# Where the later conditioning rows are kept, and which tile pairs are turned by transfers, in a conditioned decoder layer

## The chip, the cores and the metric

The kernel runs on one core of a Trainium2 chip. Its engines work side by side: TensorE (PE) multiplies, VectorE (DVE) and ScalarE (ACT) work on elements, GpSimd (POOL) only issues a few transfers, and SyncE (SP) issues nearly all transfers from HBM. Each engine takes its own instructions in order and waits on semaphores for the others. The metric is the time of one execution in microseconds on the device. Three executions of the kernel before took 2380.26, 2380.55 and 2392.89 us: the median is 2380.55 us. All of it is measured with the kernel's weights in float32.

## The reference, cut to what matters

One layer over 256 tokens of width 2048: a SwiGLU feed-forward, a pair of token mixers (retention, and attention in a window), and a second SwiGLU feed-forward, each behind an RMS norm. The norms are shifted and scaled, and the results gated, by nine vectors that come from a condition `c`.

```python
c_act = silu(c)
mod = (c_act @ w_ada + b_ada).reshape(1, 9, 2048)      # nine vectors, 151 MB of weights
h = modulate(rms_norm(x, norm_ffn1), mod[:, 0], mod[:, 1])
x = x + 0.5 * mod[:, 2] * swiglu(h, w_ffn1_gu, w_ffn1_down)      # 2048 -> 2 x 5632 -> 2048
h = modulate(rms_norm(x, norm_mix), mod[:, 3], mod[:, 4])
x = x + mod[:, 5] * token_mixing(h, w_in, w_ret_branch, w_swa_branch, w_out, sinks)
h = modulate(rms_norm(x, norm_ffn2), mod[:, 6], mod[:, 7])
x = x + 0.5 * mod[:, 8] * swiglu(h, w_ffn2_gu, w_ffn2_down)
return rms_norm(x, norm_final)

def token_mixing(h, ...):
    rq, rk, rv, rg, sq, sk, sv, gl_ret, gl_swa = split(h @ w_in)
    y_ret = (silu(rg) * group_rms(retention(rotary(rq), rotary(rk), rv))) @ w_ret_branch
    y_swa = windowed_attention_with_sinks(sq, sk, sv) @ w_swa_branch
    return (sigmoid(gl_ret) * y_ret + sigmoid(gl_swa) * y_swa) @ w_out
```

## The kernel before

**Products.** Every matrix product is made in three matmuls of a reduced float32 format: the float32 operand is split into a high half and the rest, and high x high, low x high and high x low are added up in PSUM (L338, L339, L341 in `products`). The 256 tokens are two tiles of 128. A weight block of four times 128 x 512 (1 MB) is loaded into one of four buffers called `raw` (`load`, L328; L964 in the first feed-forward's first part). `split` makes its halves two chunks at a time: ScalarE casts the high half `wh` (L351), VectorE subtracts to get `wl` (L353). One weight block is two splits and 24 matmuls. `gemm_part` walks one block for each column group; `gemm` goes over all of K.

**Order.** SP's queue is in the order of the code. The other engines' instructions are ordered by a scheduler ahead of time, except in two stretches whose order is written by hand. A `raw` buffer is loaded again when VectorE has made the second `wl` of the block that was in it, four loads earlier.

**Conditioning rows.** `c_act @ w_ada` is not done on TensorE. The weights lie transposed, and a row is 128 x 2048 (1 MB): 128 outputs. VectorE multiplies it with `c_act` and sums, in four passes of 512 (`ada_pass`, L206). There are 144 rows, 16 for each vector. `conditioning` is a generator with one pass a step; `tick`, called for each half block, runs it at the rate that `set_pace` sets. A row's place comes from `place()`, and its load (`ada_load`, L201) is put into SP's queue `pace["ahead"]` passes ahead of its first pass. There are two kinds of places. `raw_row` takes the next of the four `raw` buffers, the ring of the weights. `two_rows` takes a big buffer (a `slot`, 2 MB) and uses its two halves in turn. The first feed-forward uses `raw_row` in its last group, and then two halves of a slot, at 1.37 passes for each half block and four passes ahead. The token mixers and the second feed-forward use `raw_row`, two passes ahead; behind the softmax heads the rate is 0.95, in the second feed-forward 64/160 = 0.4.

**Tiles that are turned.** After a SwiGLU pair (one gate and one up product of 512 columns) the result must be transposed to be the next product's operand. `transpose_to` does this on TensorE, four 128 x 128 transposes for each of two token tiles (L479), and ScalarE copies them out of PSUM (L480). `turn_by_dma` does it by transfer: ScalarE copies the two 16-bit halves of the words apart (L496), SP issues a transposing transfer (L501), and ScalarE puts the halves together (L512). `later` spreads these steps over ten blocks; `turn_step` runs one step of each open turn after each block.

**Stages,** with the start of the first load of each in the profiled execution: the first feed-forward's first eight pairs of columns in four groups over K (its last group, the only one with turned pairs, is issued from about 290 us on), its last three pairs from 372 us, its down projection from 499 us, the projection to the mixers from 731 us (first keys and values, then queries, rotary and values, with the softmax heads and the retention as side work, then gates and `rg`), the branch projections with gates from 1274 us, `w_out` from 1547 us, the second feed-forward's up projection to 2120 us, and its down projection to the end. `soft`, which holds the logits of the softmax heads, lies in the place of `x_sb` (tag `x`); x is written to HBM before (`x_d`, L1051) and read back by POOL (L1376) when the place is free.

Of the kernel before, what the change touches and what calls it, by code (L numbers as in the profile page):

```python
# [9 lines left out]
F32 = mybir.dt.float32  # L10
# [7 lines left out]
P = 128  # L18
S = 256
D = 2048  # L20
DFF = 5632
# [3 lines left out]
CH = 512  # L25
# [3 lines left out]
EARLY = 8  # L29
# [48 lines left out]
def layer_kernel(  # L78
# [25 lines left out]
    one = ctx.enter_context(tc.tile_pool(name="one", bufs=1))  # L104
# [33 lines left out]
    def slot():  # L138
        return slots.tile([P, KD * S], F32, tag="slot", name=nm("slot"))
# [55 lines left out]
    AQ = 4  # L195
# [33 lines left out]
        raw = raws.tile([P, KB, CH], F32, tag="raw", name=nm("raw"))  # L229
        return raw.rearrange("p k n -> p (k n)")  # L230

    def two_rows():

        both = slot()
        turn = [both[:, :D], both[:, D:]]

        def place():
            turn.append(turn.pop(0))
            return turn[-1]

        return place
# [59 lines left out]
    turns = []  # L301
# [581 lines left out]
    gu, dn = w_ffn1_gu[0], w_ffn1_down[0]  # L883
# [125 lines left out]
    for g, ks in enumerate(groups):  # L1009
        final = g == len(groups) - 1  # L1010
        if final:
            set_pace(ROWS_FFN1, 32 * 192 // 32, place_row, 1)
        order = chunks if (len(groups) - g) % 2 else chunks[::-1]
        coming = iter(()) if final else group(groups[g + 1])
        due = 0 if final else 2 * len(groups[g + 1])
        stay = () if final else order[-2:]
        for i, n in enumerate(order):
            visit(n, ks, n not in stay, final)
            if final:
                turn_step()  # L1020
            last = len(order) - 2
            for _ in range((i + 1) * due // last - i * due // last if i < last else i == last):
                next(coming, None)
            if n in stay:
                continue
            if not final:
                to_parts(n)
            elif n % 2:
                swiglu_up(
                    banks.pop(n - 1),  # L1030
                    banks.pop(n),
                    tiles,
                    n // 2,
                    (part_of(n - 1), part_of(n)),
                    n // 2 in (1, 5),
                )
    gate = gate_row()
    tiles.append(slot())
    row_ring.append(two_rows())
    pace["rate"] = (192 - 32) / 117  # L1040
    pace["ahead"] = AQ
    ffn_up(held, gu, tiles, EARLY, turned=range(EARLY, DFF // CH - 1))
    gate_in = gate_load(gate, 2)
    wi = w_in[0]
    held, head, ahead, *calls = into_norm(3, wi, O_SK, O_SV)
# [6 lines left out]
    soft = one.tile([P, NT * D], F32, tag="x", name="soft")  # L1052
    planes_of = one.tile([P, D], F32, tag="row", name="planes_of")
    RATE_SOFT, RATE_AFTER = 0.25, 0.95
    set_pace([(7, 2, None), (6, None, None), (5, None, 1.0)], 192 / 0.95, raw_row, 2)

    def in_chunk(c0):
        return gemm(held, wi, [c0])[0]
# [142 lines left out]
    def softmax_heads():  # L1201

        turned = {}
        for at in range(4 * (QUADS + 1) + 2):
            g, part = divmod(at, 4)
            if part == 0 and g < QUADS:
                quad_weights(g)
            if part == 1 and g >= 2:
                quad_values(g - 2)
            if part == 2 and g >= 1:  # L1210
                turned[g - 1] = quad_turn()
            if part == 2 and g < QUADS:
                quad_apart()
            if part == 3 and g >= 1:
                quad_together(turned.pop(g - 1))
                if g == QUADS:
                    dec.append(one.tile([P, D], F32, tag="row", name="dec"))
                    nc.gpsimd.dma_start(dec[0], consts[:, C_DEC:])
            yield
        pace["rate"] = RATE_AFTER  # L1220

    for ci in range(4):
        b = in_chunk(O_SQ + ci * CH)
# [157 lines left out]

    gate = gate_row()
    tiles = [slot() for _ in range(3)]
    set_pace([(8, None, 0.5)], 160, raw_row, 2)
    ffn_up(held, w_ffn2_gu[0], tiles, 0, head, range(DFF // CH - 1), ahead)
    gf = one.tile([P, KD * S], F32, tag="hh", name="gf")[:, :D]
    spare = one.tile([P, 2, KD * P], F32R, tag="hl", name="spare")
    nc.gpsimd.dma_start(gf, norm_final[None, :].broadcast_to([P, D]))
# [107 lines left out]
```

## Time and profile before

| what | value |
|---|---|
| three runs, median | 2380.55 us (2380.26 to 2392.89) |
| profiled execution | 2393.78 us; span of the core 2392.0 us, mean granted clock 0.997 |
| TensorE busy | 2351.4 us |
| VectorE / ScalarE busy | 1702.1 / 1310.0 us |
| moved by DMA | 625.78 MB, 262 GB/s in the mean |
| rows loaded into `raw` / into a slot (1 MB each) | 73 / 67, landing 5.5 / 7.1 us after issue (median) |
| transposing transfers at L501 | 62, landing 6.6 us after issue (median) |
| transposes on TensorE at L479 | 72 |

In rows of instructions stand the line, the engine, the operation, out<-in by the program's names, the count, then busy time in us and mean ns of one, and then the idle time of the engine before them with what ended it. In rows of a timeline the first number is the start in us from the span's start, the second the duration, and a bracket tells how long the engine stood idle before and what released it. In rows of waits stand the total in us, the number of waits and the longest. In rows by window stand the window, its length, the busy time of PE, of its weight loads, of DVE, ACT and POOL with counts, the granted clock, the DMA engines' busy share, and GB/s. The chain that ended last is almost wholly TensorE's matmuls at L338, L339 and L341.

### The profile page before, as it was taken

The page shows a single profiled execution, that of the slowest core. Times are in us where ns is not written, and L with a number is a line of the kernel's source. Part 1 is how long each engine was busy: PE and PEld are TensorE (multiplying, and loading weights), DVE is VectorE, ACT ScalarE, POOL GpSimd, SP SyncE. Part 2 cuts the span into 40 slices and gives each one's busy share as a digit, 9 for nine tenths or more (in the row PEclk, how much of TensorE's full clock was granted, in tenths as well). Part 3 has the DMA queues.
Part 4 walks back from the last instruction along what each step waited for, and adds up shares of the span by engine and source line. Part 5 has one row for each costly group of instructions (what it writes and reads, how often), then busy time and mean ns, then how long its engine had stood idle before and what let it go on. Part 6 is the DMA issues. An engine that isn't in the chain of part 4 may idle for free. (4 is left out here: it accounts for less than half of the span.)

```text
span 2392.0 us, 28418 instructions
## 1 busy us (share of the span) xinstructions
PE 2351.4 (98%) x10470; PEld 1924.5 (80%) x10470; DVE 1702.1 (71%) x2635; ACT 1310.0 (55%) x1792; POOL 7.7 (0%) x18
## 2 busy tenths in 40 slices
PE   7999999999999999999999999999999999999998
PEld 5788888888788888778887787887888888888886
DVE  6887799778877768976776676767655555545656
ACT  6553456454546568774555464466445445454544
POOL 0000000000000000000000000000000000000000
PEclk9999999999999999999999999999999999999999
DMA  9977789998876789867689797755667877765553
GB/s 354 367 278 277 265 284 342 349 339 316 321 255 236 279 270 247 253 213 286 248 278 293 236 299 282 272 195 192 237 238 237 254 247 246 255 220 194 183 204 124
DMA packets 177581, 625.78 MB, mean 262 GB/s; under 512 B 100321, under 2 KB 100705, under 8 KB 106913
## 3 DMA queue, kind: packets, MB, share of 16 engines
q1 hardware_dynamic: 175362, 613.11, 74.4%
q0 software_dynamic: 1504, 9.81, 1.0%
q8 instruction: 82, 1.34, 0.2%
q10 hardware_dynamic: 576, 1.05, 0.1%
q14 instruction: 57, 0.47, 0.1%
HBM read 597.16 MB, written 4.22 MB: 251 GB/s over the span
## 5 line engine op out<-in xcount | busy, mean ns | idle before, releaser
L351 ACT CAST wh<-raw 128x1024 fp32r<-128x1024 f32 x794 | 834.0, 1053 | 927.1 <-PE pa L339 895.4
L353 DVE TENSOR_TENSOR wl<-raw,wh 128x1024 fp32r<-128x1024 f32 x794 | 964.2, 1223 | 524.6 <-ACT wh L351 522.3
L338 PE MATMUL pa<-wh,hh 128*128 128x512 f32 x2192 | 855.4, 391 | 3.3 <-ACT wh L351 3.3
L339 PE MATMUL pa<-wh,hl 128*128 128x512 f32 x2192 | 854.5, 390 | 0.2 <-DVE hl L601 0.2
L341 PE MATMUL pa<-wl,hh 128*128 128x512 f32 x2192 | 778.2, 392 | 1.4 <-DVE wl L353 1.3
L338 PEld LDWEIGHTS pa<-wh,hh 128*128 128x128 f32 x2192 | 411.9, 188 | 93.6 <-ACT wh L351 5.3
L341 PEld LDWEIGHTS pa<-wl,hh 128*128 128x128 f32 x2192 | 409.9, 188 | 90.4 <-DVE wl L353 4.3
L339 PEld LDWEIGHTS pa<-wh,hl 128*128 128x128 f32 x2192 | 412.1, 188 | 85.2 <-DVE hl L601 0.4
L339 PE MATMUL pa<-wh,a 128*128 128x512 f32 x944 | 365.8, 390 | 0.4 <-DVE a L387 0.4
L341 PE MATMUL pa<-wl,a 128*128 128x512 f32 x944 | 351.0, 392 | 9.4 <-DVE wl L353 9.4
L338 PE MATMUL pa<-wh,a 128*128 128x512 f32 x944 | 350.7, 392 | 1.7 <-DVE t L607 1.1
L206 DVE CUSTOM_DVE_ANT_0 raw<-raw,cact 128x512 f32<-128x512 f32 (+1 forms) x296 | 189.8, 695 | 65.5 <-DMA raw<-in_w_ada_dram 59.4
L341 PEld LDWEIGHTS pa<-wl,a 128*128 128x128 f32 x944 | 177.3, 188 | 49.9 <-DVE wl L353 13.5
L338 PEld LDWEIGHTS pa<-wh,a 128*128 128x128 f32 x944 | 178.0, 189 | 40.3 <-DVE t L607 1.9
L339 PEld LDWEIGHTS pa<-wh,a 128*128 128x128 f32 x944 | 177.8, 188 | 37.9 <-DVE a L387 1.0
L206 DVE CUSTOM_DVE_ANT_0 slot<-slot,cact 128x512 f32<-128x512 f32 (+1 forms) x216 | 170.0, 835 | 5.1 <-DMA slot<-in_w_ada_dram 4.8
L512 ACT COPY slot<-back 128x512 uint16<-128x512 uint16 x124 | 82.7, 766 | 0.0
L387 DVE TENSOR_TENSOR a<-slot,a 128x512 fp32r<-128x512 f32 x118 | 80.5, 684 | 0.0
L386 ACT CAST a<-slot 128x512 fp32r<-128x512 f32 x118 | 72.7, 617 | 1.9 <-DVE t L671 1.9
L496 ACT COPY flat<-t 128x512 uint16<-128x512 uint16 x112 | 63.5, 616 | 8.1 <-DVE t L1344 5.5
L206 DVE DVE_READ_ACCUMULATOR2_ANT sums<- 128x1 f32 x512 | 42.2, 82 | 0.0
L996 DVE TENSOR_TENSOR slot<-slot,pa 128x512 f32<-128x512 f32 x48 | 31.9, 683 | 3.2 <-PE pa L341 3.1
(205 smaller groups left out, 1143.1 us busy)
## 6 DMA issues: line engine op xcount, KB each, us to landing
raw<-in_w_ffn_gu_dram SPq DMA_DIRECT2D x160, 1024.0 KB, 5.2
raw<-in_w_in_dram SPq DMA_DIRECT2D x104, 1024.0 KB, 5.7
raw<-in_w_ffn_down_dram SPq DMA_DIRECT2D x88, 1024.0 KB, 4.9
raw<-in_w_ada_dram SPq DMA_DIRECT2D x73, 1024.0 KB, 5.5
slot<-in_w_ada_dram SPq DMA_DIRECT2D x67, 1024.0 KB, 7.1
raw<-in_w_ffn_gu_dram SPq DMA_DIRECT2D x32, 512.0 KB, 5.5
raw<-in_w_swa_branch_dram SPq DMA_DIRECT2D x16, 1024.0 KB, 5.1
raw<-in_w_ret_branch_dram SPq DMA_DIRECT2D x16, 1024.0 KB, 5.0
```

The lines of the kernel that those rows point to most:

```text
L206: nc.vector.tensor_tensor_reduce(out=w[:, at], in0=w[:, at], in1=cact[:, at], scale=1.0, scalar=0.0, op0=ALU.mult, op1=ALU.add, accum_out= ...
L338: nc.tensor.matmul(ps, ah[:, j, ts], wh[:, j, :], start=first, stop=False)
L339: nc.tensor.matmul(ps, al[:, j, ts], wh[:, j, :], start=False, stop=False)
L341: nc.tensor.matmul(ps, ah[:, j, ts], wl[:, j, :], start=False, stop=last).ins
L351: cast.append(nc.scalar.copy(hi, src).ins)
L353: low.append(nc.vector.tensor_sub(lo, src, hi.bitcast(F32)).ins)
L386: nc.scalar.copy(hi, v)
L387: nc.vector.tensor_sub(lo, v, hi.bitcast(F32))
L496: nc.scalar.copy(planes[:, i, :], words(src)[:, :, i])
L512: nc.scalar.copy(into[:, :, :, i], held["turned"][:, i])
L996: nc.vector.tensor_add(p, p, b)
```

## The change

There are three parts.

- *More turned pairs.* In the first feed-forward's last group the pairs 1, 3, 5 and 7 are turned by transfers, where it was 1 and 5; of the pairs 8, 9 and 10 behind it all three, where it was 8 and 9; in the second feed-forward all eleven, where it was the first ten. So four pairs, with 32 transposes, leave TensorE, and eight transposing transfers are added.
- *Rows of the mixers.* Behind the softmax heads (which end in the projection `w_in`), after seven more blocks and in the step of the eighth, a tile `rows_x` is made in the place of `soft`, and rows go to its two halves, loaded four passes ahead. Until then they use the `raw` ring as before. The rate is the same.
- *Rows of the second feed-forward.* They go to two halves of the fourth slot, four passes ahead, at 64/150 = 0.427 a half block and starting five passes' worth later.

```diff
-    def two_rows():
-
-        both = slot()
+    def two_rows(both=None):
+
+        both = slot() if both is None else both
...
-                    n // 2 in (1, 5),
+                    n // 2 % 2 == 1,
...
-    ffn_up(held, gu, tiles, EARLY, turned=range(EARLY, DFF // CH - 1))
+    ffn_up(held, gu, tiles, EARLY, turned=range(EARLY, DFF // CH))
...
-    set_pace([(7, 2, None), (6, None, None), (5, None, 1.0)], 192 / 0.95, raw_row, 2)
+    row_ring.clear()
+    set_pace([(7, 2, None), (6, None, None), (5, None, 1.0)], 192 / 0.95, place_row, 2)
+
+    def rows_beside():
+
+        for _ in range(7):
+            yield
+        row_ring.append(two_rows(one.tile([P, 2 * D], F32, tag="x", name="rows_x")))
+        pace["ahead"] = AQ
...
         pace["rate"] = RATE_AFTER
+        turns.append(rows_beside())
...
-    set_pace([(8, None, 0.5)], 160, raw_row, 2)
-    ffn_up(held, w_ffn2_gu[0], tiles, 0, head, range(DFF // CH - 1), ahead)
+    set_pace([(8, None, 0.5)], 150, two_rows(), AQ)
+    pace["due"] = -5.0
+    ffn_up(held, w_ffn2_gu[0], tiles, 0, head, range(DFF // CH), ahead)
```

**Where instructions move.** First, SP's queue in the first feed-forward, where the last group ends and the next part begins (`in_w_ffn_gu` are weight blocks, `in_w_ada` rows). Before:

```order
L964 DMA raw_2920<-in_w_ffn_gu_dram 128x2048
L964 DMA raw_2958<-in_w_ffn_gu_dram 128x2048
L201 DMA raw_2993<-in_w_ada_dram 128x2048
L964 DMA raw_3027<-in_w_ffn_gu_dram 128x2048
L964 DMA raw_3068<-in_w_ffn_gu_dram 128x2048
L201 DMA raw_3103<-in_w_ada_dram 128x2048
L328 DMA raw_3133<-in_w_ffn_gu_dram 128x2048
L201 DMA slot_3130<-in_w_ada_dram 128x2048
```

The same place after the change:

```order
L964 DMA raw_2914<-in_w_ffn_gu_dram 128x2048
L964 DMA raw_2952<-in_w_ffn_gu_dram 128x2048
L201 DMA raw_2987<-in_w_ada_dram 128x2048
L964 DMA raw_3021<-in_w_ffn_gu_dram 128x2048
L501 DMA_TRANSPOSE back_3057<-flat_2792 128x8x128
L964 DMA raw_3064<-in_w_ffn_gu_dram 128x2048
L201 DMA raw_3099<-in_w_ada_dram 128x2048
L501 DMA_TRANSPOSE back_3102<-flat_2857 128x8x128
L328 DMA raw_3119<-in_w_ffn_gu_dram 128x2048
L201 DMA slot_3116<-in_w_ada_dram 128x2048
```

The two transfers of pair 3 now stand between the weight blocks, one ahead of the last row of the ring and one ahead of the first row of the slot.

Second, SP's queue in the branch projections, for the same weight blocks and the same row (`raw_10521` before; after, the second row of `rows_x` shown). Before:

```order
L328 DMA raw_10400<-in_w_swa_branch_dram 128x2048
L201 DMA raw_10435<-in_w_ada_dram 128x2048
L328 DMA raw_10442<-in_w_swa_branch_dram 128x2048
L501 DMA_TRANSPOSE back_10478<-flat_10269 128x8x128
L328 DMA raw_10486<-in_w_swa_branch_dram 128x2048
L201 DMA raw_10521<-in_w_ada_dram 128x2048
L501 DMA_TRANSPOSE back_10524<-flat_10310 128x8x128
```

After (`raw_10436` is the block that was `raw_10442`):

```order
L201 DMA rows_x<-in_w_ada_dram 128x2048
L328 DMA raw_10396<-in_w_swa_branch_dram 128x2048
L328 DMA raw_10436<-in_w_swa_branch_dram 128x2048
L201 DMA rows_x<-in_w_ada_dram 128x2048
L501 DMA_TRANSPOSE back_10473<-flat_10265 128x8x128
L328 DMA raw_10481<-in_w_swa_branch_dram 128x2048
L501 DMA_TRANSPOSE back_10517<-flat_10307 128x8x128
```

The row's load moves ahead of one weight block and one transposing transfer, and the weight blocks have the four `raw` buffers to themselves.

Third, VectorE at that row's first pass (`a` are halves of the other operand, made at L387). Before:

```order
L353 TENSOR_TENSOR wl_10379<-raw_10359,wh_10378 128x1024
L353 TENSOR_TENSOR wl_10403<-raw_10400,wh_10402 128x1024
L387 TENSOR_TENSOR a_10394<-slot_6360,a_10394 128x512
L353 TENSOR_TENSOR wl_10420<-raw_10400,wh_10419 128x1024
L206 ISA raw_10521,sums_9253<-raw_10521,cact 128x512
```

The row's buffer is that of the block `raw_10400`, four loads of the ring earlier, whose second split stands right ahead of the row's first pass. After:

```order
L353 TENSOR_TENSOR wl_10289<-raw_10268,wh_10288 128x1024
L353 TENSOR_TENSOR wl_10319<-raw_10316,wh_10318 128x1024
L353 TENSOR_TENSOR wl_10336<-raw_10316,wh_10335 128x1024
L387 TENSOR_TENSOR a_10310<-slot_6366,a_10310 128x512
L353 TENSOR_TENSOR wl_10357<-raw_10354,wh_10356 128x1024
L387 TENSOR_TENSOR a_10313<-slot_6366,a_10313 128x512
L353 TENSOR_TENSOR wl_10375<-raw_10354,wh_10374 128x1024
L206 ISA rows_x,sums_9259<-rows_x,cact 128x512
```

The load of the block ahead of this row in SP's queue (`raw_10436`) waits for the split of `raw_10268`; four splits stand between that and the row's first pass. The half of `rows_x` that the row is loaded into was last read earlier still. POOL's order stays: the load of x ahead of the write of gate 5.

## The prediction

> **What bounds the kernel now.** I read the page first, then busy time by windows, then the waits of TensorE and of VectorE, and then the timelines around TensorE's longest wait.
>
> ```profile
> span 2392.0 us, 28418 instructions
> PE 2351.4 (98%) x10470; PEld 1924.5 (80%) x10470; DVE 1702.1 (71%) x2635; ACT 1310.0 (55%) x1792; POOL 7.7 (0%) x18
> ```
>
> TensorE (PE) is busy in 98% of the span, so a change gains in only two ways: fewer TensorE instructions, or less of the 2392.0 - 2351.4 = 40.6 us in which it stands still. The second way needs the places where it waits in the middle of the program:
>
> ```profile
> PE pa L341 <- DVE wl L353: 4.2, 4, 2.2
> ```
> ```profile
> PE pa L341 <- DVE wl L353: 2.0, 1, 2.0
> ```
> ```profile
> PE pa L341 <- DVE wl L353: 1.8, 1, 1.8
> ```
>
> These are TensorE's waits in 1260-1345, 1350-1365 and 1480-1500 us of the span (total, count, longest): 4.2 + 2.0 + 1.8 = 8.0 us, each time for the low half of a weight block (`wl`, made by VectorE at L353). They all lie in the branch projections and the gates. What made VectorE late is on its own timeline, with the queue that issues its data and with TensorE behind it:
>
> ```profile
> 1308.31 0.33 SPq L328 DMA_DIRECT2D raw<-in_w_swa_branch_dram  x1
> 1311.19 0.33 SPq L201 DMA_DIRECT2D raw<-in_w_ada_dram  x1
> 1311.57 1.34 SPq L501 DMA_TRANSPOSE back<-flat  x1
> ```
> ```profile
> 1315.22 1.22 DVE L353 TENSOR_TENSOR wl<-raw,wh 128x1024 fp32r<-128x1024 f32 x1 [0.91 <-ACT wh L351]
> 1319.12 0.69 DVE L206 CUSTOM_DVE_ANT_0 raw<-raw,cact 128x512 f32<-128x512 f32 x1 [2.67 <-DMA raw<-in_w_ada_dram]
> ...
> 1321.57 1.22 DVE L353 TENSOR_TENSOR wl<-raw,wh 128x1024 fp32r<-128x1024 f32 x1
> ```
> ```profile
> 1322.85 0.72 PE L341 MATMUL pa<-wl,a 128*128 128x512 f32 x2 [2.18 <-DVE wl L353]
> ```
>
> A conditioning row is issued at 1311.19 and VectorE, which runs in order, stands 2.67 us until it lands. Four passes over it follow (1319.12 to 1321.57, 2.45 us), and the split that TensorE needs is behind them; TensorE stands 2.18 us. So it is the row that is late, not the weight block. The same two groups on the page, and VectorE's waits for rows in 1200-1530 and in 420-640, tell where rows go wrong:
>
> ```profile
> L206 DVE CUSTOM_DVE_ANT_0 raw<-raw,cact 128x512 f32<-128x512 f32 (+1 forms) x296 | 189.8, 695 | 65.5 <-DMA raw<-in_w_ada_dram 59.4
> ...
> L206 DVE CUSTOM_DVE_ANT_0 slot<-slot,cact 128x512 f32<-128x512 f32 (+1 forms) x216 | 170.0, 835 | 5.1 <-DMA slot<-in_w_ada_dram 4.8
> ```
> ```profile
> DVE raw L206 <- DMA raw<-in_w_ada_dram: 34.7, 17, 3.3
> ```
> ```profile
> DVE slot L206 <- DMA slot<-in_w_ada_dram: 1.4, 3, 0.5
> ```
>
> Rows in the ring of weight buffers (`raw`) cost VectorE 59.4 us of waiting, rows in two halves of a slot 4.8 us; 34.7 us of the first fall in 1200-1530. The stalls have a second price, the granted clock:
>
> ```profile
> 1260.00:1320.00 60.00, 57.57 (x250) 46.36 (x249) 41.11 (x70) 37.22 (x49) 0.00 (x0) 1.00 1.00 291
> 1320.00:1330.00 10.00, 7.82 (x27) 5.95 (x27) 6.35 (x11) 2.65 (x4) 0.00 (x0) 0.83 0.79 291
> 1360.00:1370.00 10.00, 9.14 (x33) 7.43 (x34) 5.59 (x6) 3.25 (x4) 0.00 (x0) 0.83 0.58 210
> ```
>
> The clock is 0.83 in the ten microseconds behind each of the two stalls of 2 us and more, which loses 2 x 10 x 0.17 = 3.4 us. [...]
>
> **Transposes off TensorE.** Four more pairs of tiles are turned by transfers: 3 and 7 in the first feed-forward's last group, 10 behind it, and 10 in the second.
>
> ```profile
> 316.57 0.39 PE L338 MATMUL pa<-wh,hh 128*128 128x512 f32 x1
> 316.80 1.03 PE L479 MATMUL ps<-small_c,t 128*128 128x128 f32 x8
> 317.59 0.48 PE L341 MATMUL pa<-wl,hh 128*128 128x512 f32 x1
> ```
>
> Matmuls start 0.23 us apart (316.57, and the next would at 316.80). One pair's eight transposes take the place of the matmul due at 316.80, and that one starts at 317.59: 0.79 us a pair, 4 x 0.79 = **-3.2 us**, on the engine that sets the time. What it costs elsewhere:
>
> ```profile
> L480 ACT COPY slot<-ps x18: 567/584/596, 317.4 to 2149.2; 128x512 f32<-128x512 f32 x18
> ```
> ```profile
> L496 ACT COPY flat<-t x112: 604/615/630, 323.4 to 2108.7; 128x512 uint16<-128x512 uint16 x112
> ```
> ```profile
> L512 ACT COPY slot<-back x124: 756/767/786, 369.6 to 2148.1; 128x512 uint16<-128x512 uint16 x124
> ```
> ```profile
> L501 SPq DMA_TRANSPOSE back<-flat x62: 1237/1330/6980, 336.2 to 2115.4; - x62
> ```
>
> ScalarE (ACT) does four copies of 0.615 and four of 0.767 us for a pair in place of two of 0.584: 5.53 - 1.17 = +4.4 us, hidden beside TensorE as long as it has idle time. SP issues eight transfers more, at 1.33 us (median) and up to 6.98 us each, with weights and rows queued behind them. The pairs 10 of both feed-forwards I take at 0, by the stretch of 420-480, in which pair 8 is turned this way already: TensorE is busy 60.00 us of 60 there. The four transfers of pairs 3 and 7 go into the stretch ahead of it:
>
> ```profile
> 300.00:360.00 60.00, 60.00 (x278) 49.86 (x277) 55.17 (x92) 34.09 (x43) 0.00 (x0) 1.00 0.87 285
> 360.00:420.00 60.00, 59.60 (x274) 48.77 (x273) 55.11 (x106) 36.88 (x49) 0.00 (x0) 1.00 0.96 339
> 420.00:480.00 60.00, 60.00 (x266) 49.58 (x266) 45.84 (x85) 26.43 (x29) 2.23 (x4) 1.00 0.98 355
> ```
> ```profile
> DVE raw L206 <- DMA raw<-in_w_ada_dram: 5.3, 5, 1.9
> ```
> ```profile
> 350.67 0.69 DVE L206 CUSTOM_DVE_ANT_0 raw<-raw,cact 128x512 f32<-128x512 f32 x1 [1.94 <-DMA raw<-in_w_ada_dram]
> ...
> 362.76 0.69 DVE L206 CUSTOM_DVE_ANT_0 raw<-raw,cact 128x512 f32<-128x512 f32 x1 [1.41 <-DMA raw<-in_w_ada_dram]
> ```
>
> ScalarE has the room (34 to 37 of 60 us). VectorE is busy 110.3 of 120 us here and waits 5.3 us for rows, so it has 4.4 us left, and DMA is busy 0.87 to 0.96. Two rows that stood beside a transfer and without one made VectorE wait 1.94 and 1.41 us: 0.53 us more. One more row of the ring and the first of the slot now have an added transfer ahead of them in SP's queue; at 0.53 us each, handed on to TensorE whole, that is **+1.1 us**. Bounds: 0, if the weights' lead takes it up, and four transfers at the longest issue, 4 x 6.98 - 4.4 = +23.5 us. I take the low one, since the only two rows of this stretch that differ in this one thing lie there.
>
> **Rows out of the ring.** From some 43 us after the last softmax head, rows go to two halves of x's place. The order shows what this does: the row's load stands one weight block earlier in SP's queue and waits for the row before last, not for the split just ahead of its own passes; four splits lie between instead of none. Splits come every 2.7 us (a block of 24 matmuls at 0.23 us holds two), so a row has some 11 us where it needed 7.9 (issued at 1311.19, there at 1319.12). Rows then arrive before VectorE asks, as in 420-640, where rows come faster (1.37 passes for each half block against 0.95) and waits add up to 1.4 us. Gain on TensorE: **-8.0 us** of waits and **-3.4 us** of clock. Bounds: 0 if the rows stay late, -11.4 if all goes. The four passes stay where VectorE is, but without the wait ahead of them the splits are some 2.5 us earlier, more than the longest stall. Late next would be the block's high half on ScalarE, which this change leaves alone.
>
> x itself can come back only when the last row is done:
>
> ```profile
> 1114.27 1.06 POOL L1376 DMA_DIRECT2D x_sb<-x_d  x2 [34.73 <-DVE sums L206]
> 1537.88 0.50 POOL L275 DMA_DIRECT2D gate_d<-t  x1 [422.56 <-ACT t L274]
> ```
> ```profile
> 1613.27 1.29 DVE L608 TENSOR_TENSOR x_sb<-x_sb,t 128x512 f32<-128x512 f32 x2
> ```
>
> Its load moves from 1114 to behind the last row's passes, which come just ahead of the write of gate 5 at 1538, on the same queue of POOL; the first reader is at 1613. I take 0: some 75 us of cover. If that cover went, VectorE would wait, then the accumulators would stay full and TensorE stop.
>
> **Rows in the fourth slot** (second feed-forward): VectorE's row waits there
>
> ```profile
> DVE raw L206 <- DMA raw<-in_w_ada_dram: 6.7, 4, 2.9
> ```
>
> are 6.7 us in 1650-2100, and none of TensorE's waits quoted above lies there. I take 0, bounds -0.5 and +0.5.
>
> **Sum.** Against the profiled execution (2393.78 us, span 2392.0): 2393.78 - 3.2 - 8.0 - 3.4 + 1.1 = 2380.3. That execution stands 13.2 us over the median of 2380.55, next to the highest of the three runs (2392.89). Taking away its stalls and clock loss alone gives 2393.78 - 11.4 = 2382.4, close to the two lower runs: so I read the low runs as those in which these rows came in time by chance. Off the median only transposes and transfers count then: 2380.55 - 3.2 + 1.1 = 2378.5. This is the likeliest time, and its own range is 2375 to 2382.
>
> **Rivals.** *Slower.* The added transfers hold up SP in 300-420, where each ring row is loaded just before its use. What is needed: the gain of 3.2 must be overcome and 11.9 us lost (0.5%, about what a measurement of this kernel can tell from no change), 15.1 us of stall; with VectorE's 4.4 us of room that is 19.5 us, or 4.9 us from each of four transfers.
>
> ```profile
> 380.01 5.61 SPq L501 DMA_TRANSPOSE back<-flat  x1
> ```
>
> For it speaks this one, which held SP 5.61 us in that stretch; against it, that TensorE lost only 0.40 us in 360-420 (59.60 busy) with two such in it. At 5.61 each: 4 x 5.61 - 4.4 = 18.0, so 2380.55 - 3.2 + 18.0 = 2395.4. [...] *Partly lost:* two such holds, or clock loss that stays: up to 2391. *The whole sum comes off the median*, because the low runs hold the same stalls and profiling cost the 13 us: 2380.55 - 13.5 = 2367.1; against it, one run without a profile is as long as the profiled one. *The rows are no earlier*: if DMA throughput (1.00 busy in 1260-1320), not order, makes them land late, the stalls stay, and the median is again 2378.5 to 2381.
>
> **Chances.** Forecast 0.60; partly lost 0.14; rows no earlier 0.07; these are within 0.5%: 0.81. Whole sum off the median: faster, 0.08. Slower 0.11. The range 2369 to 2391 leaves out the last two, 0.19.
>
> **What would show it.** Rows named for x's place with VectorE's waits for them under 5 us in 1200-1530 (34.7 now); no TensorE wait over 1 us there and a clock of 1.00; 32 transposes fewer at L479; row waits in 300-420 between 5 and 7 us. I am wrong if those go over 10 us, if TensorE idles by more than 3 us in 300-480, or if x's rows show waits like those of the ring.

## The result, and the profile after

The changed kernel takes 2376.41 us (median of 20 runs, 2373.17 to 2382.16). The kernel before, timed beside it, takes 2385.34 us (median of 20 runs, 2380.26 to 2392.89): the ratio is 0.9964, 95% interval 0.9956 to 0.9971, or -8.9 us. That is less than the 0.5% named in the prediction, but the interval lies clear of 1. The profiled execution took 2376.93 us; that of before, 2393.78 us, is longer than every run of it on record, so the two profiles lie 16.9 us apart, and not all of that is the typical gain.

First the head of the page after, and VectorE's three groups of passes over rows (ring, x's place, slots):

```profile
span 2375.2 us, 28320 instructions
...
PE 2342.6 (99%) x10438; PEld 1921.9 (81%) x10438; DVE 1702.5 (72%) x2635; ACT 1322.7 (56%) x1816; POOL 7.7 (0%) x18
...
L206 DVE CUSTOM_DVE_ANT_0 slot<-slot,cact 128x512 f32<-128x512 f32 (+1 forms) x280 | 210.3, 800 | 12.5 <-DMA slot<-in_w_ada_dram 12.5
...
L206 DVE CUSTOM_DVE_ANT_0 raw<-raw,cact 128x512 f32<-128x512 f32 (+1 forms) x108 | 70.7, 706 | 21.2 <-DMA raw<-in_w_ada_dram 14.9
L206 DVE CUSTOM_DVE_ANT_0 rows_x<-rows_x,cact 128x512 f32<-128x512 f32 x124 | 78.7, 687 | 9.7 <-DMA rows_x<-in_w_ada_dram 9.3
```

There are 32 matmuls fewer (10470 to 10438): the transposes of four pairs. Waits for rows sum to 12.5 + 14.9 + 9.3 = 36.7 us, where 59.4 + 4.8 = 64.2 us stood before. VectorE's waits for rows, first in 1200-1530, then in 300-420 us of the span (total, count, longest):

```profile
DVE rows_x L206 <- DMA rows_x<-in_w_ada_dram: 8.6, 12, 1.9
```
```profile
DVE raw L206 <- DMA raw<-in_w_ada_dram: 4.6, 5, 2.3
```

The 34.7 us of 1200-1530 became 8.6, and the 5.3 us of 300-420 became 4.6. TensorE waits for nothing in 1200-1530. Its waits in 300-480 and in 420-700 are these:

```profile
PE pa L341 <- DVE wl L353: 0.9, 1, 0.9
```
```profile
PE pa L341 <- DVE wl L353: 2.4, 1, 2.4
```

The second is new as a single wait: before, TensorE lost 1.48 us there, in three pieces. By windows (PE, its weight loads, VectorE, ScalarE and POOL busy, with counts, then clock, DMA share and GB/s), stretches that the prediction showed, the one around the new wait, and the whole of 1200-1530:

```profile
360.00:420.00 60.00, 59.14 (x268) 48.43 (x267) 54.48 (x101) 40.34 (x55) 0.00 (x0) 1.00 1.04 348
...
1260.00:1320.00 60.00, 60.00 (x266) 49.64 (x265) 45.30 (x77) 38.16 (x51) 0.00 (x0) 1.00 0.91 318
1320.00:1330.00 10.00, 10.00 (x46) 8.29 (x45) 8.60 (x18) 6.50 (x10) 0.00 (x0) 1.00 0.76 295
1360.00:1370.00 10.00, 10.00 (x46) 8.29 (x45) 7.29 (x14) 4.89 (x6) 0.00 (x0) 1.00 0.71 301
640.00:650.00 10.00, 7.57 (x27) 5.85 (x26) 10.00 (x19) 5.21 (x12) 0.00 (x0) 0.84 0.56 211
```
```profile
1200.00:1530.00 330.00, 329.97 (x1457) 272.94 (x1456) 243.38 (x402) 182.15 (x228) 2.10 (x4) 1.00 0.81 293
```

The two stretches that held the stalls of 2 us are full and at a clock of 1.00; the only place below full clock, up to the last few microseconds, is now at 647 to 650 us (0.84 in 640-650, 0.99 in the ten microseconds behind). The last row is the one that the experiments are compared by: 1457 matmuls in 330 us is one each 0.2265 us, TensorE's full pace. The same row of the profiled execution of before:

```profile
1200.00:1530.00 330.00, 320.13 (x1387) 261.26 (x1386) 234.58 (x400) 174.01 (x218) 0.00 (x0) 0.99 0.83 278
```

It has 70 matmuls fewer; at 0.2265 us these are 15.9 us, nearly the whole 16.9 us between the two profiles. (Two profiles further below in which TensorE is busy for the whole 330.00 us, the mixers' rows alone and the one with more turned pairs, count 1457 and 1459 matmuls in this window, so a difference of two is not read.)

### The profile page after: what moved, and what is told of

Same layout as the page of the kernel before. It is cut to its first block, busy times and chain, and to the rows that moved or that the text cites. A ratio compares the mean times of both kernels' runs of the same rounds, so it can differ in the third digit from the quotient of the medians.

```text
span 2375.2 us, 28320 instructions
## 1 busy us (share of the span) xinstructions
PE 2342.6 (99%) x10438; PEld 1921.9 (81%) x10438; DVE 1702.5 (72%) x2635; ACT 1322.7 (56%) x1816; POOL 7.7 (0%) x18
## 4 chain that ended last, share of the span: by engine, by line
PE 94%; DVE 2%; DMA 2%; issue 1%; ACT 0%; SPq 0%; DVEq 0%; ACTq 0%
PE pa L341 31%; PE pa L338 31%; PE pa L339 31%; DMA raw<-in_w_ada_dram 1%; DVE wl L353 1%; PE ps L1201 0%; DMA x_sb<-in_x_dram 0%; DVE raw L206 0%; PE pd L1117 0%; DMA raw<-in_w_ffn_gu_dram 0%; DVE slot L206 0%; ACT wh L351 0%; PE ps L817 0%; DVE t L607 0%; PE ps L1117 0%
## 5 line engine op out<-in xcount | busy, mean ns | idle before, releaser
L206 DVE CUSTOM_DVE_ANT_0 slot<-slot,cact 128x512 f32<-128x512 f32 (+1 forms) x280 | 210.3, 800 | 12.5 <-DMA slot<-in_w_ada_dram 12.5
L512 ACT COPY slot<-back 128x512 uint16<-128x512 uint16 x140 | 93.4, 766 | 0.0
L206 DVE CUSTOM_DVE_ANT_0 raw<-raw,cact 128x512 f32<-128x512 f32 (+1 forms) x108 | 70.7, 706 | 21.2 <-DMA raw<-in_w_ada_dram 14.9
L206 DVE CUSTOM_DVE_ANT_0 rows_x<-rows_x,cact 128x512 f32<-128x512 f32 x124 | 78.7, 687 | 9.7 <-DMA rows_x<-in_w_ada_dram 9.3
L387 DVE TENSOR_TENSOR a<-slot,a 128x512 fp32r<-128x512 f32 x118 | 80.6, 684 | 0.3
L496 ACT COPY flat<-t 128x512 uint16<-128x512 uint16 x128 | 72.7, 617 | 3.0 <-DVE t L1274 2.6
```

The lines of the kernel that those rows point to most:

```text
L206: nc.vector.tensor_tensor_reduce(out=w[:, at], in0=w[:, at], in1=cact[:, at], scale=1.0, scalar=0.0, op0=ALU.mult, op1=ALU.add, accum_out= ...
L387: nc.vector.tensor_sub(lo, v, hi.bitcast(F32))
L496: nc.scalar.copy(planes[:, i, :], words(src)[:, :, i])
L512: nc.scalar.copy(into[:, :, :, i], held["turned"][:, i])
```

## Experiments

Each of the first eight kernels below was timed against the kernel before on the same chip. The three parts alone and the first of the two kernels with a hold share one chip, where before took 2385.49 us (median of 23 runs); the other four share another, with 2387.22 us (21 runs). Ratios can be compared between the chips, times less well. The last three executions are of unchanged kernels, one each, on a third chip.

### Turned pairs alone

```diff
-                    n // 2 in (1, 5),
+                    n // 2 % 2 == 1,
...
-    ffn_up(held, gu, tiles, EARLY, turned=range(EARLY, DFF // CH - 1))
+    ffn_up(held, gu, tiles, EARLY, turned=range(EARLY, DFF // CH))
...
-    ffn_up(held, w_ffn2_gu[0], tiles, 0, head, range(DFF // CH - 1), ahead)
+    ffn_up(held, w_ffn2_gu[0], tiles, 0, head, range(DFF // CH), ahead)
```

> Only the four more turned pairs, rows as in the kernel before. Theory: TensorE loses 32 transposes, 3.2 us, and the added transfers cost it next to nothing in 300-420 us of the span; against that stands the one wait of 2.4 us at 647 that the changed kernel's trace has and the kernel before has in three smaller pieces (1.5 us in all), with some 1.6 us of lowered clock behind it. Sum: 3.2 - 0.9 - 1.6 = 0.7 us less, between 0 and 3.5 less, and the stalls for late rows in 1200-1530 stay, 8 us or so in the profile. Rival, transfers hold up the queue: 2 us or more longer than the kernel before, with VectorE's row waits in 300-420 well over 5 us.

Measured: 2382.12 us (11 runs), ratio 0.9987 (0.9978 to 0.9996), -3.1 us at the ratio. The stretch with the four added transfers, then the one around 647 us, and TensorE's wait in 420-700:

```profile
360.00:420.00 60.00, 60.00 (x274) 49.76 (x273) 54.37 (x99) 41.23 (x56) 0.00 (x0) 1.00 1.05 345
...
640.00:650.00 10.00, 7.56 (x34) 5.94 (x33) 10.00 (x21) 5.92 (x13) 0.00 (x0) 1.00 0.55 211
```
```profile
PE pa L341 <- DVE wl L353: 2.4, 1, 2.4
```

TensorE loses nothing beside the transfers (60.00 of 60). The theory held and the slower rival fell. A delay of rows by the transfers does not show: VectorE's row waits of 300-420 came to 0.6 us in this execution, and to 0.6 to 5.9 us in the seven profiles of kernels without the added transfers. And the single wait of 2.4 us at 647 us comes with the turned pairs, since neither the rows' new place nor the slot is in this kernel. Here, where TensorE sets the time and ScalarE has room (busy 41.23 of the 60 us above), moving four pairs away from TensorE gained 3.1 us.

### Rows of the mixers in x's place, alone

```diff
-    def two_rows():
-        both = slot()
+    def two_rows(both=None):
+        both = slot() if both is None else both
...
+    def rows_beside():
+        for _ in range(7):
+            yield
+        row_ring.append(two_rows(one.tile([P, 2 * D], F32, tag="x", name="rows_x")))
+        pace["ahead"] = AQ
...
+        turns.append(rows_beside())
```

> Only the mixers' rows moved to x's place, nothing else. Theory: this is where the time went: VectorE's row waits in 1200-1530 fall from 34.7 to under 10 us, TensorE waits there no longer for any low half, and the time falls by 6 to 9 us. Rival, most of the 9 us came from the transposes and the two other parts: the time falls by less than 4 us.

Measured: 2377.09 us (5 runs), ratio 0.9964 (0.9952 to 0.9976), -8.4 us between the medians: practically the whole effect of the change. TensorE's row by window, and VectorE's waits for rows in it:

```profile
1200.00:1530.00 330.00, 330.00 (x1457) 272.70 (x1456) 242.91 (x402) 181.42 (x227) 2.10 (x4) 1.00 0.81 293
```
```profile
DVE rows_x L206 <- DMA rows_x<-in_w_ada_dram: 15.6, 14, 2.1
```

TensorE is at full pace for 330 us, although VectorE still waits 15.6 us for rows, where under 10 us was expected: the time came as forecast, the sign for it did not. That the weight blocks have the four `raw` buffers to themselves is not what gains, as far as the traces tell: in 1200-1530 ScalarE, which reads a block first, has no wait for a block's transfer in this kernel, nor in any of the three executions of the kernel before.

### Rows of the second feed-forward in the fourth slot, alone

```diff
-    set_pace([(8, None, 0.5)], 160, raw_row, 2)
+    set_pace([(8, None, 0.5)], 150, two_rows(), AQ)
+    pace["due"] = -5.0
```

> Only the second feed-forward's rows in the fourth slot, at the later start and the higher rate. Theory: no difference, within 1 us, since TensorE had no long wait there. Rival: rows in the ring cost TensorE something in this stage too that the one profile did not show, 2 us or more less.

Measured: 2383.93 us (11 runs, 2379.76 to 2391.59), ratio 0.9993 (0.9982 to 1.0005): no difference shown. Its profiled execution (2381.30 us) is worth more than the verdict, because up to 1530 us it is the kernel before in one of its short executions. By window, then VectorE's row waits and TensorE's waits for low halves in 1200-1530:

```profile
1200.00:1530.00 330.00, 326.88 (x1435) 268.02 (x1434) 241.97 (x406) 178.47 (x223) 0.96 (x2) 1.00 0.82 284
```
```profile
DVE raw L206 <- DMA raw<-in_w_ada_dram: 14.3, 16, 2.5
```
```profile
PE pa L341 <- DVE wl L353: 2.1, 4, 0.8
```

Rows wait only 14.3 us here, against 34.7 us in the profiled execution of before, and the stalls of 2 us are absent; yet it is 1457 - 1435 = 22 matmuls, or 5.0 us, short of full pace. Two of the small waits, with VectorE's first and last pass ahead of them and the split behind:

```profile
1336.70 0.68 DVE L206 CUSTOM_DVE_ANT_0 raw<-raw,cact 128x512 f32<-128x512 f32 x1
...
1338.53 0.68 DVE L206 CUSTOM_DVE_ANT_0 raw<-raw,cact 128x512 f32<-128x512 f32 x1
...
1339.75 1.22 DVE L353 TENSOR_TENSOR wl<-raw,wh 128x1024 fp32r<-128x1024 f32 x1
```
```profile
1339.88 0.50 PE L338 MATMUL pa<-wh,a 128*128 128x512 f32 x1 [0.44 <-DVE slot L1360]
1341.02 0.73 PE L341 MATMUL pa<-wl,a 128*128 128x512 f32 x2 [0.40 <-DVE wl L353]
```

The first pass has no bracket: no row is late. TensorE waits because the four passes stand between one gating product of VectorE (L1360, it empties an accumulator) and the next, with the split behind them. This pair of waits recurs in the three profiled executions of the kernel before (0.44 and 0.41 us or 0.40 at 1344 to 1348 us) and in none of the three with early rows in x's place (this part alone, and the changed kernel twice), where the passes stand elsewhere among the splits. So a part of the gain, some 0.85 us of idle time, is VectorE's order, not the rows' arrival.

### x's place, but rows loaded one pass ahead

The second part alone again, with rows loaded one pass ahead instead of four. The ring has two, so in passes this is later than before; in time the lead is about the ring's, as the table further below shows.

```diff
         row_ring.append(two_rows(one.tile([P, 2 * D], F32, tag="x", name="rows_x")))
-        pace["ahead"] = AQ
+        pace["ahead"] = 1
```

> The mixers' rows in x's place, but their loads are put into SP's queue one pass ahead instead of four. The order still has three splits between what SP waits for and a row's first pass, where the ring had none or one. Theory, what counts is that a row no longer takes a buffer of the weights' ring: as with the mixers' rows alone, 6 to 9 us less than the kernel before, VectorE's row waits in 1200-1530 under 20 us. Rival, what counts is the earlier load: row waits stay at 25 us or more and at most 4 us are gained.

Measured: 2384.31 us (11 runs), ratio 0.9984 (0.9975 to 0.9993), -3.8 us at the ratio, under half of the gain.

```profile
1200.00:1530.00 330.00, 325.65 (x1423) 266.80 (x1422) 240.29 (x405) 177.86 (x224) 1.55 (x3) 0.99 0.81 288
```
```profile
DVE rows_x L206 <- DMA rows_x<-in_w_ada_dram: 29.9, 16, 3.7
```

VectorE's waits are nearly those of the ring (34.7 us at the most), and 34 matmuls are missing. The theory that the place alone does it fell; the rows also have to be loaded earlier. What the 3.8 us consist of is not shown by this one execution.

### The ring, but rows loaded earlier

The kernel before, with rows of the ring eight passes ahead behind the softmax heads.

```diff
         pace["rate"] = RATE_AFTER
+        pace["ahead"] = 2 * AQ
```

> Rows stay in the weights' ring, but from the end of the softmax heads on their loads stand in SP's queue eight passes ahead instead of two; the rest is the kernel before. In the order a row still waits for a split right ahead of its first pass. Theory, the ring is the cause: no gain, within 2 us of the kernel before or longer, row waits in 1200-1530 at 15 to 35 us as before, and TensorE's waits for low halves stay. Rival, the earlier load is enough: 5 us less or more, and row waits under 10 us.

Measured: 2389.86 us (11 runs), ratio 1.0009 (1.0000 to 1.0018): no gain, as the theory had it.

```profile
1200.00:1530.00 330.00, 322.75 (x1407) 265.48 (x1406) 236.60 (x396) 176.59 (x223) 1.05 (x2) 0.99 0.81 283
```
```profile
DVE raw L206 <- DMA raw<-in_w_ada_dram: 31.2, 18, 5.1
```

Why neither half of this part does the whole alone is told in part by the time that a row has. From the traces, each row's load is paired with its four passes for the rows used in 1270-1520 (medians in us): how long after issue VectorE asks for it, and how long after issue it has landed.

| kernel | asked after | landed after | VectorE's waits for these rows, sum |
|---|---|---|---|
| before (profiled execution) | 5.0 | 6.7 | 28.9 |
| before, again 1 (further below) | 5.3 | 5.5 | 19.1 |
| before, again 2 (further below) | 5.3 | 5.4 | 12.5 |
| ring, eight passes ahead | 5.4 | 6.7 | 19.1 |
| x's place, one pass ahead | 5.9 | 7.1 | 22.5 |
| x's place, four ahead (alone) | 7.3 | 7.4 | 13.3 |
| the changed kernel | 7.5 | 7.3 | 3.7 |
| the changed kernel, again | 7.5 | 7.2 | 9.3 |

In the ring an earlier place in SP's queue buys 0.1 to 0.4 us, because the load still waits for a ring buffer to be read: in 1200-1530 SP stands 52.3 us, in 22 waits, ahead of row loads until a split is made. Place and earlier load together buy 2 us and more over the ring (1.4 us of it by the earlier load), which is about what is needed and little above it. The sum of VectorE's waits does not decide: 13.3 us cost TensorE nothing in x's place, while 12.5 us in the ring went with 36 matmuls fewer.

### More turned pairs

The changed kernel with the pairs 0, 2, 4 and 6 of the first feed-forward turned by transfers too.

```diff
-                    n // 2 % 2 == 1,
+                    True,
```

> The changed kernel, with the pairs 0, 2, 4 and 6 of the first feed-forward's last group turned by transfers too, so that all its eight pairs are: sixteen transposing transfers in some 90 us in place of eight. Theory: TensorE loses another 32 transposes, 3.2 us, but each of the sixteen stands in SP's queue ahead of rows and weights, and the three buffers between ScalarE's two steps are now waited for: row waits in 300-420 rise to 10 us or more and TensorE waits 5 us or more there, so the time is 2 to 10 us longer than the changed kernel. Rival, transfers stay free: 3 us less than the changed kernel, no new wait in 300-420.

Measured: 2377.00 us (5 runs), ratio 0.9958 (0.9946 to 0.9971): the same as the changed kernel. Both expectations fell, the one of a loss and the one of 3 us more. TensorE's timeline at the two longest of its new waits, and the window of the second:

```profile
394.08 0.73 PE L341 MATMUL pa<-wl,hh 128*128 128x512 f32 x2 [1.00 <-DVE wl L353]
```
```profile
534.37 0.60 PE L339 MATMUL pa<-wh,a 128*128 128x512 f32 x1 [2.21 <-DVE a L387]
```
```profile
530.00:540.00 10.00, 7.79 (x28) 5.79 (x27) 6.65 (x14) 4.00 (x6) 0.00 (x0) 0.83 1.00 388
```

The 3.2 us taken off TensorE came back as 1.00 + 2.21 us of waits and 10 x 0.17 = 1.7 us of clock, besides two new waits of 0.7 us, while the stall at 647 us is absent in this execution. The further turns moved the stall and gained nothing that these runs resolve.

### The stall at 647 us

In the changed kernel, VectorE's timeline at the stall and TensorE's:

```profile
639.37 1.21 DVE L353 TENSOR_TENSOR wl<-raw,wh 128x1024 fp32r<-128x1024 f32 x1
...
642.90 0.68 DVE L206 CUSTOM_DVE_ANT_0 slot<-slot,cact 128x512 f32<-128x512 f32 x1
...
645.35 1.22 DVE L353 TENSOR_TENSOR wl<-raw,wh 128x1024 fp32r<-128x1024 f32 x1
```
```profile
646.62 1.12 PE L341 MATMUL pa<-wl,a 128*128 128x512 f32 x2 [2.44 <-DVE wl L353]
```

Between two splits, 5.98 us apart, stand four of the products and sums that empty the accumulators (L607 and L608, 640.50 to 642.90) and four passes (642.90 to 645.35); no instruction waits. Before, the same work stood between two splits 5.99 us apart, but with the passes ahead of the sums, and TensorE then lost 0.61 + 0.47 + 0.40 us. Two kernels hold passes back at this place (7 or 5 passes' worth at the first down projection) and run the rows a little faster before it.

```diff
         banks = gemm(act, w, [0, CH], KT=KT)
+        pace["due"] -= pace.pop("hold", 0.0)
...
-    pace["rate"] = (192 - 32) / 117
+    pace["rate"] = (192 - 32) / 110
+    pace["hold"] = 7.0
```

> The changed kernel, and besides the conditioning steps of the first feed-forward are held back by seven passes where its down projection's first accumulators are emptied, and run at 160/110 instead of 160/117 passes a half block to make up for it, so that no four passes stand between two splits there. Theory: the wait of 2.4 us at 647 and the lowered clock behind it go, 2.5 to 4 us less than the changed kernel, so 11 to 13 us less than the kernel before. Rival: the wait there belongs to the emptying of the accumulators itself and stays, or the higher rate fills the DMA engines and moves the wait elsewhere: no difference to the changed kernel, 9 us less than the kernel before.

Measured with 7: 2377.79 us (6 runs), ratio 0.9964 (0.9951 to 0.9978). The stall at 647 us and its lowered clock are gone and other waits came, so the theory fell and the rival held; the largest is 1.73 us, for a low half, at 379 us.

The second kernel has the rate at 160/114 and the hold at 5:

```diff
-    pace["rate"] = (192 - 32) / 117
+    pace["rate"] = (192 - 32) / 114
+    pace["hold"] = 5.0
```

> The changed kernel with the conditioning steps of the first feed-forward held back by five passes at the emptying of the first accumulators, and a rate of 160/114 instead of 160/117. Theory: the wait of 2.4 us at 647 goes without the waits at 380 and 535 that the higher rate of 160/110 brought; 2 to 4 us less than the changed kernel. Rival: any higher rate brings waits elsewhere, and the time is that of the changed kernel within 1.5 us.

Measured: 2376.11 us (5 runs), ratio 0.9955 (0.9942 to 0.9967). Its largest new wait is 1.45 us, again for a low half, at 377 us.

No stretch is below full clock up to 2360 us, and its profiled execution took 2374.20 us, but the interval overlaps that of the changed kernel (0.9956 to 0.9971): if it is better, then by less than these runs resolve.

### The same kernels again

What the prediction assumed of the short runs was put to the test with further executions of unchanged kernels.

> The kernel before, unchanged, profiled again. The prediction held that its executions of 2380 us have none of the stalls behind late rows and those of 2393 us have all. If that is so, the profiled span is either near 2379 with TensorE's waits for the low half in 1200-1530 under 1 us, or near 2392 with about 8 us of them. Rival: rows are late in every execution and only the amount varies; then the waits lie between 2 and 8 us and the span goes with them, some 2379 to 2392, and half-clock stretches come only with waits near 2 us and more.

> The same kernel once more, so that three executions of it can be set side by side: the span less the waits of TensorE and less 1.7 us for each half-clock stretch should be the same within 2 us in all three if the stalls are what varies; if it differs by more, something else (the start, for one) varies too.

The first took 2386.85 us, the second 2388.35 us. By window, with the first and the second in that order, and VectorE's waits for rows in 1200-1530 in the same order:

```profile
1200.00:1530.00 330.00, 324.32 (x1421) 265.47 (x1421) 240.77 (x405) 178.59 (x223) 0.00 (x0) 1.00 0.83 284
```
```profile
1200.00:1530.00 330.00, 324.01 (x1421) 265.50 (x1420) 241.27 (x411) 178.73 (x222) 0.00 (x0) 1.00 0.83 285
```
```profile
DVE raw L206 <- DMA raw<-in_w_ada_dram: 23.6, 16, 3.2
```
```profile
DVE raw L206 <- DMA raw<-in_w_ada_dram: 15.5, 11, 3.4
```

Both are 36 matmuls, or 8.2 us, short of full pace. That is the gain of 8.4 us measured for the mixers' rows. The theory of two kinds of execution (all stalls or none) fell and its rival held: rows are late in every one, and only the amount varies. The rival's last clause fell, though: in both executions the clock was lowered behind the three pieces at 644 to 649 us, none of them near 2 us. The whole account, from the traces: TensorE's idle time behind the start (the first 26 us), how much of it lies in 1200-1530, half-clock stretches (1.7 us each), and the span less idle time and these.

| execution | span | idle | in 1200-1530 | half-clock stretches | span less these | matmuls short in 1200-1530 |
|---|---|---|---|---|---|---|
| before, profiled | 2392.0 | 16.4 | 9.9 | 2 | 2372.2 | 70 |
| before, again 1 | 2385.0 | 11.8 | 5.7 | 1 | 2371.5 | 36 |
| before, again 2 | 2386.5 | 12.3 | 6.0 | 1 | 2372.5 | 36 |
| fourth slot alone | 2379.5 | 8.9 | 3.1 | 0 | 2370.6 | 22 |

The three of the kernel before agree within 1.0 us once stalls and clock are taken off, so it is the stalls that vary. The idle time understates the loss: 36 matmuls are 8.2 us, but 5.7 and 6.0 us are seen as idle. In the profile's rows a matmul lasts 0.39 us and the next starts 0.23 us behind it, so a wait also ends an overlap of 0.16 us, and in the row at 1339.88 above the first matmul behind one lasts 0.50 us.

> The changed kernel, profiled again. If the stall at 647 us belongs to the change, TensorE waits about 2.4 us for one low half there again, and in 1200-1530 not at all; the span is near 2375. If it was chance, the wait is again in pieces of 0.4 to 0.7 us and the span some 2 to 3 us shorter.

It took 2378.28 us (span 2376.5). By window:

```profile
1200.00:1530.00 330.00, 329.69 (x1455) 272.24 (x1454) 243.03 (x405) 182.05 (x229) 2.11 (x4) 1.00 0.81 292
```

The stall at 647 us is there again, a single wait of 2.4 us, as expected if it belongs to the change, and 1200-1530 is full again but for 0.3 us. VectorE's row waits there came to 16.3 us, twice those of the first profile.

## Why the prediction came out as it did

**Time and direction.** Forecast 2378.5, measured 2376.41, in the likeliest case's own range (2375 to 2382). That it came so close is luck, since two errors nearly cancelled: the base was 4.8 us too low (2380.55 of three runs against 2385.34 of twenty), and the gain was -8.9 where "off the median" only -3.2 + 1.1 was counted.

**The step that failed** is the reading of the two low runs as "those in which these rows came in time by chance". Of the 20 runs of the kernel before, they are the two lowest (2380.26 and 2380.55), and even an execution of 2381.30 us in the ring's arrangement lacks 22 matmuls, 5.0 us. The two further ones, of 2386.85 and 2388.35 us and so nearer to the median, lack 36, or 8.2 us. So most of the stalls' worth does come off the median. The rival "the whole sum comes off the median" gave half of the right reason (low runs hold stalls too), but its time, 2367.1, took the stalls of the longest run as those of all and set out from the low base.

**Rows out of the ring: -8.0 and -3.4.** The mechanism was right: with this part alone the waits are gone, the clock is 1.00 and -8.4 us is measured. For the profiled execution the term was sized too small: TensorE was 15.9 us behind there, not 11.4. Waits of some 0.4 us each (1.9 us in all, two of them from VectorE's order and not from rows) were not counted, and some 2.6 us are the overlap lost at each wait, which the profile counts as busy; the prediction's "only two ways" left it out. For an execution nearer to the median the term was too large: in the two further ones no stretch of 1200-1530 is at half clock, so the 3.4 us of clock were not there to gain.

**"A row has some 11 us where it needed 7.9."** It has 7.5 us, and needs 7.3 in the median. The four splits are there, but not 2.7 us apart. The row of the order shown ahead of the prediction, in the changed kernel:

```profile
1299.99 0.43 SPq L201 DMA_DIRECT2D rows_x<-in_w_ada_dram  x1
```
```profile
1298.36 3.49 DVE L353 TENSOR_TENSOR wl<-raw,wh 128x1024 fp32r<-128x1024 f32 x3
...
1307.55 0.69 DVE L206 CUSTOM_DVE_ANT_0 rows_x<-rows_x,cact 128x512 f32<-128x512 f32 x1 [0.34 <-DMA rows_x<-in_w_ada_dram]
```

The first of three splits in a row, made back to back behind the passes of the row before, lets SP go on; the four splits behind it are done by 1307.21, 7.6 us later and not 11. Rows therefore still come late: waits of 8.6 and 16.3 us where under 5 was expected. They no longer reach TensorE, but for 0.3 us in the second profile. Shorter single waits (2.3 us at the longest, 3.2 to 3.4 in the three executions of before) are not the whole of it, since what a wait costs depends on where it stands:

```profile
1305.75 0.69 DVE L206 CUSTOM_DVE_ANT_0 raw<-raw,cact 128x512 f32<-128x512 f32 x1 [1.14 <-DMA raw<-in_w_ada_dram]
```
```profile
1268.03 0.69 DVE L206 CUSTOM_DVE_ANT_0 rows_x<-rows_x,cact 128x512 f32<-128x512 f32 x1 [3.84 <-DMA rows_x<-in_w_ada_dram]
```

The first, in the kernel before, was followed by a wait of TensorE of 0.89 us; the second, in the kernel with a hold of 7, by none until another row came 2.16 us late (then 0.79 us). The passes stand elsewhere among the splits; how the gain divides between earlier rows and that order was not separated.

**Four turned pairs: -3.2.** Alone they gave -3.1 us. The +1.1 us for rows beside the added transfers did not appear: row waits in 300-420 were 4.6 us, and 0.6 us with the turns alone, where 5.3 stood and 5 to 7 was given as the sign, and TensorE idled 0.9 us in 300-480, below the 3 us named as a sign of error. But on top of the mixers' rows no gain is resolved: both ratios are 0.9964, and the interval of the mixers' rows alone (0.9952 to 0.9976) is too wide to exclude one of 3 us. In the profiles of these two kernels, 2375.1 and 2375.2 us long, the turns' gain is given back. They bring the single wait at 647 us (2.44 against 1.48 us in three pieces) and, in both profiles of the changed kernel, a half-clock stretch behind it, together 2.7 us of the 3.2; a wait at 377 us that grew from 0.40 to 0.86 us makes up the rest. With the turns alone the same 2.44 us stand without lowered clock in the one profile, so -3.1 us was measured with this wait included. (The three pieces cost such a stretch too in both further executions of the kernel before, but not in the first, nor with the mixers' rows alone.) No term of the sum stood for a change of VectorE's order so far behind the edit.

**The slower rival** needed the transfers to hold SP in 300-420; TensorE was busy 60.00 of 60 us beside them in the kernel with the turns alone. **Rows no earlier**, because DMA throughput decides: fell, with 0.91 busy in 1260-1320 and full pace. **Late next on ScalarE**: not so; in 1200-1530 nothing over 0.3 us is late next, and elsewhere it is VectorE's low half.

**x back later: 0.** Right. POOL's load and the first reader on VectorE:

```profile
1504.99 1.05 POOL L1385 DMA_DIRECT2D x_sb<-x_d  x2 [425.02 <-PE pa L341]
```
```profile
1597.57 1.28 DVE L608 TENSOR_TENSOR x_sb<-x_sb,t 128x512 f32<-128x512 f32 x2
```

The load is issued 92.6 us ahead of its reader, which does not wait. **Rows in the fourth slot: 0.** Right within the interval, 0.9982 to 1.0005.

## What to carry to other kernels

As these runs show it, a side load that shares a ring of buffers with the main stream is not made early by moving its issue alone (5.4 us from issue to use, where 5.0 to 5.3 stood), since its buffer is freed only just ahead; give it a place of its own and an earlier issue together (7.3 to 7.5 us), and measure the lead as issue to use against issue to landing. When a few runs differ by more than the effect, profile a short one too before taking it for the clean case, and count matmuls in a fixed window rather than idle time (36 matmuls or 8.2 us were seen as 5.7 and 6.0 us of it). On a program that one engine sets, work taken off it can be given back where another engine's order is tight (here 2.7 of 3.2 us, at 647 us), so look for stalls far behind the edit.

## What was unexpected of the hardware

The same gap does not always cost clock. The wait of 2.44 us at 647 us took the granted clock to 0.84 in 640-650 in the changed kernel, but with the turned pairs alone the same 2.44 us left it at 1.00 (both rows are shown above). The reverse in the kernel before, first execution again: a wait of 1.70 us at 1488.8 left the clock alone, and three pieces of 0.61, 0.47 and 0.40 us within 3 us, at 644 to 647, cost it.

The traces show most of what decides. In the nine of the thirteen profiles that have half-clock stretches in the middle of the program, each lasts 3.41 us, and the time at full clock ahead of it, counted from some 30 us on, is a whole number of steps of 3.413 us: 617.81 us or 181 steps in the changed kernel, 1269.76 or 372 with the turned pairs alone, 1293.65 or 379 in the kernel before. So in these profiles the clock changes on a grid of that step, and a wait counts by what falls into one step of it. The step of the wait and the next, in the changed kernel, then with the turned pairs alone, and last the two steps of the first execution again:

```profile
643.34:646.76 3.42, 0.98 (x5) 0.52 (x4) 3.42 (x10) 1.03 (x3) 0.00 (x0) 1.00 1.00 424
646.76:650.17 3.41, 3.41 (x9) 2.64 (x10) 3.41 (x7) 1.60 (x5) 0.00 (x0) 0.50 0.10 38
```
```profile
642.06:645.47 3.41, 1.86 (x9) 1.20 (x7) 3.41 (x11) 1.67 (x3) 0.00 (x0) 1.00 0.99 411
645.47:648.89 3.42, 2.53 (x11) 2.12 (x12) 3.42 (x5) 1.29 (x5) 0.00 (x0) 1.00 0.41 170
```
```profile
644.04:647.46 3.42, 1.94 (x7) 0.90 (x7) 3.42 (x6) 1.88 (x5) 0.00 (x0) 1.00 1.01 426
...
1487.14:1490.55 3.41, 1.72 (x7) 1.42 (x8) 3.38 (x5) 0.00 (x0) 0.00 (x0) 1.00 0.58 163
```

In the changed kernel the whole wait of 2.44 us lies in one step, and the next is at half clock. With the turned pairs alone the grid cuts the same wait into 1.55 and 0.89 us, and the clock stays. In the same way the two stalls of the prediction (2.18 and 2.04 us) lay in one step each, and the wait of 1.83 us at 1493 us of that profile, which cost no clock, was cut into 0.84 and 0.99 us. Over the thirteen profiles, all nine steps with 1.84 us of idle time or more were followed by half clock, and none with 1.29 us or less. Of the ten between, only two were, with 1.36 and 1.48 us, both at the three pieces; what decides there stays open.

Behind the first 30 us the longest gap in the thirteen profiles is 2.44 us, and in the changed kernel the clock falls behind a step in which TensorE is busy for 0.98 of 3.42 us.
